# A two-layer hybrid encoder: decay constants on GpSimd, decay by Exp, gates between projection tiles, paired value products

## The chip, the cores and the metric

The kernel runs on one core of one Trainium2 chip. The metric is the device time of one execution in microseconds; the kernel before takes 1383.24 us (median of 3 runs, 1381.23 to 1383.26). TensorE, VectorE (DVE), ScalarE (ACT) and GpSimd (POOL) are the engines that compute, SyncE (SP) issues nearly all loads.

## The reference, cut to what matters

A sequence of 256 tokens of width 1024 goes through two layers in float32. Each layer is a token mixer, a LayerNorm, a channel mixer, a LayerNorm. The channel mixer of the first layer is a dense SwiGLU of width 3584, that of the second the top 2 of 8 SwiGLU experts. The part that the change touches is the mixer, and in it the recurrence:

```
z = x @ W_in -> [conv B | C | h] [c_q | c_kv | k_rope] [lru gate | lru input]
xc  = depthwise_conv4(lru_input) + b
rec = sigmoid(xc @ W_a + b_a);  inp = sigmoid(xc @ W_i + b_i)     (two directions)
log_a = -8 * rec * softplus(-lam)
a = exp(log_a);  u = sqrt(-expm1(2 * log_a)) * inp * xc
h = scan(a, u);  y_lru = gelu(g) * (h_forward + h_backward)
attention: softmax(q k^T) v, 8 heads of 64
y = rms_norm of each group, concatenated, @ W_out
```

The kernel writes sigmoid by Tanh, and with c = 4 softplus(-lam) and s = tanh(c (1 + tanh(ga / 2))) it has a = 2 / (1 + s) - 1 and 1 - a^2 = s (2 / (1 + s))^2 (before), where after the change a = exp(-2c (1 + tanh)) and sqrt(1 - a^2) = sqrt(s) (1 + a).

## The kernel before, in words

All weights stream through a ring of 1 MB tiles (`fresh`, 7 buffers, and a few more in the expert stage) in a fixed order, two pieces of 1024 columns to a tile. A load is issued on SP as soon as the piece order asks for it (`ahead`, `take`) and its buffer is free. Nearly every piece is split into a high part in fp32r, cast by ScalarE (L178) or, for the indices in `HI_POOL`, by GpSimd (L176), and a low part, subtracted by VectorE (L185). A product of two split operands is three matmuls (`mm`, L104). Within the compute part the order is written by hand: `manual_schedule` keeps each engine's instructions in program order, so an instruction that waits holds up all behind it on its engine.

`boundary(i)` is the LayerNorm with the transposition for the next stage. For each of the two blocks of 128 tokens it takes the statistics (`stats`, with the power for the inverse deviation on GpSimd, L249), then applies them: the second half of block 0 on ScalarE and GpSimd (L372 to L375), the rest by two VectorE instructions per half (`centre` L256, `shift` L261). TensorE transposes (`turn`), ScalarE and VectorE copy out (`bring`, L394, L396), and `native` already multiplies the first two raw pieces into the bank `first`. `boundary(0)` also computes the decay constants c of both layers from lam: four operations on GpSimd with a power of e (L279 to L284), and a rational series on VectorE (`decay_rest`, L289 to L302).

`mixer(l)` begins with the convolution of the recurrence's input (L509 to L515), then projects zq 0 and 1, takes the gate weights, `gates(0)`, zq 2, `gates(1)`, Sqrt, two zkv tiles, zkr, and both norms (`rms_scale`, `bcast_cols`). Each `zgroup` takes a piece and runs 24 matmuls. `gates(d)` runs the gate products, four Tanh (L556) and two more Tanh for s (L562). Work of the recurrence is queued in `later` and let in by `tick`: four reciprocals (L575), two gate inputs (L578 to L582), two scans, a sum. Eight projection tiles (`filler`) are spread over the attention's heads. In the loop over heads `scores`, `flip` (the transposition of the probabilities), `softmax`, `normalise` and `values` alternate with them; `values(h)` runs two products of 64 columns, one per 128 keys, into the lower or upper half of a bank.

`dense` and `moe` follow. The expert stage starts with the routing, and its loads (336 tiles) follow in the order of the experts, four light steps of expert 0 first.

Of the kernel before, what the change touches and what calls it, by code (L numbers as in the profile page):

```python
# [29 lines left out]
PIECE = 1024  # L30

PP_CONVW, PP_QG, PP_KVG, PP_LCW, PP_LCB = 0, 6, 9, 11, 19
HI_POOL = (1, 3, 5, 6, 7, 8, 10)
MIX_KINDS = [0] * 2 + [PIECE] * 2 + [0] + [PIECE] * 6 + [768] + [PIECE] * 2 + [768] + [PIECE] * 2 + [768] + [PIECE] * 2 + [768] + [PIECE] * 10

PP_BA, PP_BI, PP_LAM, PP_MG, PP_L = 21, 25, 29, 33, 41
# [45 lines left out]
def hybrid_encoder_kernel(ctx, tc, x_in, pp_in, lnr_in, tab_in, wa_in, wm_in, out):  # L82
# [129 lines left out]
    for b in range(NB):  # L212
        t = state.tile([P, D], F32, name=f"x{b}")
        nc.sync.dma_start(out=t, in_=x_in[b * P:(b + 1) * P, :])
        xs.append(t)

    def load_rows(i, eng=nc.gpsimd):
        t = lnp.tile([P, 2 * D], F32, name="lnrows", tag="lnrows")
# [4 lines left out]
    for j in range(2):  # L223
        nc.sync.dma_start(out=rows0[:, j, 512:], in_=lnr_in[j:j + 1, 512:].to_broadcast([P, 512]))
        rows[0, j] = rows0[:, j, :]
# [6 lines left out]
    G.memset(mhalf, -0.5)  # L232
    ebase = consts.tile([P, 1], F32, name="ebase")
    G.memset(ebase, float(np.e))

    stat = {}

# [32 lines left out]
            shift(b, h, i)  # L270

    cdec = consts.tile([P, 8], F32, name="cdec")
    hbias = consts.tile([P, 2, 8], F32, name="hbias")

    def decay_consts():
        lam = consts.tile([P, 8], F32, name="lam")
        for l in range(2):
            o = l * PP_L
            G.tensor_scalar(lam[:, 4 * l:4 * l + 4], pp[:, o + PP_LAM:o + PP_LAM + 4], -1.0, 0.0, op0=OP.mult, op1=OP.add)  # L279
        na = consts.tile([P, 8], F32, name="nabs")  # L280
        G.tensor_scalar(na, lam, -1.0, 0.0, op0=OP.mult, op1=OP.add)
        V.tensor_tensor(na, na, lam, op=OP.min)
        t = consts.tile([P, 8], F32, name="texp")
        G.tensor_tensor(t, ebase.to_broadcast([P, 8]), na, op=OP.pow)  # L284
        return lam, t

    def decay_rest(lam, t):
        for l in range(2):
            V.tensor_scalar_mul(hbias[:, l, :], pp[:, l * PP_L + PP_BA:l * PP_L + PP_BA + 8], 0.5)  # L289
        s = consts.tile([P, 8], F32, name="sat")  # L290
        V.tensor_scalar_add(s, t, 2.0)
        V.reciprocal(s, s)
        V.tensor_tensor(s, s, t, op=OP.mult)
        z = consts.tile([P, 8], F32, name="zat")
        V.tensor_tensor(z, s, s, op=OP.mult)
        acc = consts.tile([P, 8], F32, name="accat")
        V.tensor_scalar_mul(acc, z, 1.0 / 17.0)
        for k in (15, 13, 11, 9, 7, 5, 3):
            V.scalar_tensor_tensor(acc, acc, 1.0 / k, z, op0=OP.add, op1=OP.mult)
        V.scalar_tensor_tensor(acc, acc, 1.0, s, op0=OP.add, op1=OP.mult)  # L300
        V.tensor_scalar(lam, lam, 0.0, 2.0, op0=OP.max, op1=OP.mult)
        V.scalar_tensor_tensor(cdec, acc, 4.0, lam, op0=OP.mult, op1=OP.add)  # L302

    def boundary(i, final=None, router=False):
        def stats(b):
# [57 lines left out]
        def keep(q):  # L363
            src, dh, dl = views(1, q)
            A.copy(dh, src)
            V.tensor_tensor(dl, src, dh.bitcast(F32), op=OP.subtract)

        stats(0)
        if final is None:
            stats(1)  # L370
        x = xs[0][:, 512:]
        A.activation(x, x, AF.Identity, bias=stat[0][2])  # L372
        A.activation(x, x, AF.Copy, scale=stat[0][1])
# [1 line left out]
        G.tensor_tensor(x, x, rows[i, 1][:, 512:], op=OP.add)  # L375
        centre(0, 0, i)
        shift(0, 0, i)
        if final is not None:
            stats(1)
        if router:  # L380
            turn(0, 0)
            turn(0, 1)
# [20 lines left out]
            native(0, y0, (1, 2))  # L403
        centre(1, 0, i)
        shift(1, 0, i)
        if i == 0:
            decay = decay_consts()
        centre(1, 1, i)
        shift(1, 1, i)
        if i == 0:  # L410
            decay_rest(*decay)
        if not router:
            for q in range(4):
                src, dh, dl = views(0, q)
# [46 lines left out]
    def mixer(l, xT, pz):  # L461
# [5 lines left out]
        with tc.tile_pool(name=f"mix{l}", bufs=1) as mx:  # L467
# [42 lines left out]
            for i in range(2):  # L510
# [35 lines left out]
            def gates(d, wgate):  # L546
                th = []
                for kind in range(2):
                    pg = bank("pg")
                    for i in range(2):  # L550
                        g0 = ((d * 2 + kind) * 2 + i) * P
                        T.matmul(pg[:, i * S:(i + 1) * S], lhsT=wgate[:, g0:g0 + P], rhs=xc[:, i * S:(i + 1) * S],
                                 start=i == 0, stop=True, skip_group_check=True)
                    t = tmp(f"th{kind}")
                    for i in range(2):
                        A.activation(t[:, i * S:(i + 1) * S], pg[:, i * S:(i + 1) * S], AF.Tanh,  # L556
                                     scale=0.5, bias=hbias[:, l, kind * 4 + d * 2 + i:kind * 4 + d * 2 + i + 1])
                    th.append(t)
                s = th[0]
                for i in range(2):  # L560
                    c = cdec[:, 4 * l + 2 * d + i:4 * l + 2 * d + i + 1]
# [8 lines left out]
            hsum = []  # L570

            def queue_recurrence():
                def inv(d, i):
                    sl = slice(i * S, (i + 1) * S)
                    V.reciprocal(rs[d][:, sl], rs[d][:, sl])  # L575

                def gate_input(d):
                    s, u, r = ss[d], us[d], rs[d]  # L578
                    V.scalar_tensor_tensor(u, u, 1.0, xc, op0=OP.add, op1=OP.mult)
                    G.tensor_tensor(s, s, r, op=OP.mult)  # L580
                    G.tensor_tensor(u, u, s, op=OP.mult)
                    G.tensor_scalar(r, r, 2.0, -1.0, op0=OP.mult, op1=OP.add)  # L582

                def scan(d):
                    u, r, h = us[d], rs[d], ss[d]
# [10 lines left out]
                    hsum.append(ss[0])  # L596

                for d in range(2):
                    for i in range(2):
                        later.append(lambda d=d, i=i: inv(d, i))  # L600
# [8 lines left out]
            def filler(i, between=None):  # L609
# [28 lines left out]
                elif i == 5:  # L638
                    gx2 = tmp("gx2")
                    A.activation(gx2, pz, AF.Square)  # L640
                    gh = tmp("gh")
                    A.activation(gh, pz, AF.Copy, scale=0.5)
# [12 lines left out]
            gates(1, wgate)  # L655
            for d in range(2):
                A.activation(ss[d], ss[d], AF.Sqrt)
            queue_recurrence()
            zkv(0)
            tick()  # L660
            zkv(1)
            tick()
            pz = bank("zkr")
            zgroup(pz[0:64, 0:S], m=64)
            kr = tmp("kr", (64, S), tag="kr", bufs=1)
# [17 lines left out]
                    V.tensor_tensor(q, pq[:, 0:S], tq, op=OP.mult)  # L683
                    qs[h] = q

            rq = rms_scale(qsq, 384, "q")
            rkv = rms_scale(kvsq, 256, "kv")
            tick()
            filler(0)
# [89 lines left out]
                A.copy(pT, pt)  # L779
                pTs[h] = pT  # L780

            yms, msq, po = [], [], [None]

            def values(h):
                k = h % 2
                if k == 0:
                    po[0] = bank("po")
                pT = pTs.pop(h)
                for j in range(NB):
                    T.matmul(po[0][64 * k:64 * k + 64, 0:S], lhsT=vt[:, j, h * 64:(h + 1) * 64],  # L790
                             rhs=pT[:, j * S:(j + 1) * S], start=j == 0, stop=j == NB - 1,
                             skip_group_check=True)
                if k == 1:
                    yms.append(scaled_pair("ym", po[0][:, 0:S], col(PP_MG + 2 + h // 2), msq))

            acc = None

# [710 lines left out]
```

## Time and profile before

| | |
|---|---|
| median of 3 runs | 1383.24 us (1381.23 to 1383.26) |
| the profiled execution | 1380.96 us |
| its span | 1379.3 us |
| busy: PE, PEld | 1343.9 us (97%), 966.6 us (70%) |
| busy: DVE, ACT, POOL | 840.6 us (61%), 671.6 us (49%), 173.0 us (13%) |
| moved by DMA | 437.73 MB, mean 317 GB/s |

PE is TensorE's matmuls, PEld its weight loads. Times of the timeline are microseconds from the span's start. A timeline row gives start, duration, engine, line, operation, output and inputs, shape and count, and in brackets how long the engine was idle before it and what ended that. Instructions of one kind in a row are merged. A float32 matmul appears as two passes.

### The profile page before, as it was taken

The page shows a single profiled execution, that of the slowest core. Times are in us where ns is not written, and L with a number is a line of the kernel's source. Part 1 is how long each engine was busy: PE and PEld are TensorE (multiplying, and loading weights), DVE is VectorE, ACT ScalarE, POOL GpSimd, SP SyncE. Part 2 cuts the span into 40 slices and gives each one's busy share as a digit, 9 for nine tenths or more (in the row PEclk, how much of TensorE's full clock was granted, in tenths as well). Part 3 has the DMA queues.
Part 4 walks back from the last instruction along what each step waited for, and adds up shares of the span by engine and source line. Part 5 has one row for each costly group of instructions (what it writes and reads, how often), then busy time and mean ns, then how long its engine had stood idle before and what let it go on. Part 6 is the DMA issues. An engine that isn't in the chain of part 4 may idle for free. (4 is left out here: it accounts for less than half of the span.)

```text
span 1379.3 us, 18986 instructions
## 1 busy us (share of the span) xinstructions
PE 1343.9 (97%) x7199; PEld 966.6 (70%) x7199; DVE 840.6 (61%) x1019; ACT 671.6 (49%) x954; POOL 173.0 (13%) x169
## 2 busy tenths in 40 slices
PE   6999999999999999999999999999999999999995
PEld 5987999999998883556665556666655666655674
DVE  7886644444589771455654555655645656544896
ACT  3763544444355621455444445554445545444674
POOL 4623311111164320000000000000000000000011
PEclk9999999999999999999999999999999999999998
DMA  8442655555074357999999999999999999999980
GB/s 324 165 179 92 228 200 184 184 184 183 31 287 151 159 208 303 421 421 421 420 421 421 421 421 421 421 421 421 420 421 421 421 421 421 421 421 409 419 356 33
DMA packets 61735, 437.73 MB, mean 317 GB/s; under 512 B 6850, under 2 KB 6978, under 8 KB 9284
## 3 DMA queue, kind: packets, MB, share of 16 engines
q1 hardware_dynamic: 60484, 432.25, 77.4%
q0 software_dynamic: 1152, 4.19, 0.9%
q8 instruction: 58, 0.95, 0.3%
q14 instruction: 41, 0.34, 0.1%
HBM read 435.37 MB, written 1.05 MB: 316 GB/s over the span
## 5 line engine op out<-in xcount | busy, mean ns | idle before, releaser
L185 DVE TENSOR_TENSOR lo<-w,hi 128x1024 fp32r<-128x1024 f32 (+1 forms) x474 | 571.1, 1244 | 55.4 <-ACT hi L178 53.3
L178 ACT CAST hi<-w 128x1024 fp32r<-128x1024 f32 (+1 forms) x462 | 471.5, 1046 | 140.8 <-DMA w<-in_wm_dram 57.0
L104 PE MATMUL gu<-hi,xg 128*128 128x512 f32 x896 | 295.6, 399 | 0.0
L1200 PE MATMUL gu<-w,xgl 128*64 128x512 f32 x896 | 205.3, 596 | 0.0
L104 PEld LDWEIGHTS gu<-hi,xg 128*128 128x128 f32 x896 | 168.6, 188 | 42.5 <-ACT hi L178 2.0
L104 PE MATMUL gu<-lo,xg 128*128 128x512 f32 x448 | 176.9, 395 | 0.2 <-DVE lo L185 0.2
L104 PE MATMUL py<-hi,hT 128*128 128x512 f32 x448 | 147.7, 400 | 0.0
L1200 PEld LDWEIGHTS gu<-w,xgl 128*64 128x64 f32 x896 | 60.9, 137 | 112.0 <-issue 110.8
L1116 ACT CAST hT<-pht 128x512 fp32r<-128x512 f32 x28 | 16.4, 585 | 230.3 <-PE pht L1111 230.3
L104 PE MATMUL gu<-xT_hi,hi 128*128 128x256 f32 x432 | 122.2, 283 | 0.0
L104 PE MATMUL gu<-xT_lo,hi 128*128 128x256 f32 x432 | 122.1, 283 | 0.0
L104 PE MATMUL gu<-xT_hi,lo 128*128 128x256 f32 x432 | 122.0, 282 | 0.0
L104 PEld LDWEIGHTS py<-hi,hT 128*128 128x128 f32 x448 | 84.3, 188 | 34.4 <-ACT hi L178 13.8
L1125 PE MATMUL py<-w,hTl 128*64 128x512 f32 x448 | 102.2, 598 | 0.0
L104 PEld LDWEIGHTS gu<-lo,xg 128*128 128x128 f32 x448 | 84.5, 189 | 18.8 <-DVE lo L185 0.5
L1117 DVE TENSOR_TENSOR hT<-pht,hT 128x512 fp32r<-128x512 f32 x28 | 19.3, 691 | 126.3 <-ACT hT L1116 126.3
L104 PE MATMUL py<-lo,hT 128*128 128x512 f32 x224 | 89.3, 399 | 2.4 <-DVE lo L185 2.3
L1215 DVE TENSOR_TENSOR h<-h,gu 128x512 f32<-128x512 f32 x28 | 19.2, 686 | 105.8 <-PE gu L104 105.8
L104 PEld LDWEIGHTS gu<-xT_hi,hi 128*128 128x128 f32 x432 | 82.6, 191 | 1.2
L104 PEld LDWEIGHTS gu<-xT_lo,hi 128*128 128x128 f32 x432 | 82.6, 191 | 1.0
L104 PEld LDWEIGHTS gu<-xT_hi,lo 128*128 128x128 f32 x432 | 82.7, 191 | 0.0
L1279 POOL TENSOR_TENSOR xl<-acc,xh 128x1024 fp32r<-128x1024 f32 x2 | 5.8, 2896 | 556.1 <-ACT xh L1278 556.1
(333 smaller groups left out, 1765.9 us busy)
## 6 DMA issues: line engine op xcount, KB each, us to landing
w<-in_wm_dram SPq DMA_DIRECT2D x336, 1024.0 KB, 15.9
w<-in_wa_dram SPq DMA_DIRECT2D x73, 1024.0 KB, 4.8
lnrows<-in_lnr_dram POOLq DMA_DIRECT2D x6, 512.0 KB, 5.2
x<-in_x_dram SPq DMA_DIRECT2D x2, 512.0 KB, 4.0
rows<-in_lnr_dram POOLq DMA_DIRECT2D x2, 512.0 KB, 10.5
out_dram<-z SPq DMA_DIRECT2D x4, 256.0 KB, 2.8
tab<-in_tab_dram SPq DMA_DIRECT2D x2, 320.0 KB, 7.5
lnrows<-in_lnr_dram SPq DMA_DIRECT2D x2, 256.0 KB, 6.4
```

Source lines behind the costliest of these rows:

```text
L104: T.matmul(dst, lhsT=a, rhs=b, start=start and i == 0, stop=stop and i == len(terms) - 1, skip_group_check=True)
L178: A.copy(hi[:, :kind], src[:, :kind])
L185: V.tensor_tensor(*todo, op=OP.subtract)
L1116: A.copy(hT[:, 0, :], pt)
L1117: V.tensor_tensor(hT[:, 1, :], pt, hT[:, 0, :].bitcast(F32), op=OP.subtract)
L1125: T.matmul(py[0][k * CAP:(k + 1) * CAP, :], lhsT=hp[:, j * CAP:(j + 1) * CAP], rhs=w[:, sl], start=first and j == 0, stop=last and j == 3, ...
L1200: T.matmul(pb[i * CAP:(i + 1) * CAP, :], lhsT=self.unit.xg[:, c, :], rhs=w[:, k * 512:(k + 1) * 512], start=c == 0, stop=c == DC - 1, skip ...
L1215: V.tensor_tensor(self.h, self.h, self.pgu[1], op=OP.mult)
L1279: G.tensor_tensor(xl[:, b], acc[0][:, b], xh[:, b].bitcast(F32), op=OP.subtract)
```

## The change

It does the following.

- At the start tile 0 of the weights is loaded behind x0, ahead of the second halves of the first LayerNorm's rows and of x1. `stats(1)` stands behind the first half of block 0 in every boundary.
- `decay_first` and `decay_rest` run on GpSimd alone, the reciprocal as a power of -1; the latter stands behind the last `keep`. It also makes cneg = -2 cdec.
- `HI_POOL` loses the indices 1 (a piece that isn't cast) and 3, so piece 3 of both mixers is cast on ScalarE.
- The convolution's taps stand behind zq 0 and zq 1, one half each. The order is then: gate weights, zq 2, `gates(0)`, zkv 0, `gates(1)`, zkv 1, Sqrt, the q norm, zkr.
- The decay is an Exp on ScalarE. The reciprocals and GpSimd's r are gone, the gate input is three VectorE operations, and two ticks between the zkv tiles are gone. GeLU's factor is 0.25.
- `values` does nothing for an even head and runs both heads of a pair at an odd one, alternating between the two halves of the bank.

```diff
-HI_POOL = (1, 3, 5, 6, 7, 8, 10)
+HI_POOL = (5, 6, 7, 8, 10)
...
         nc.sync.dma_start(out=t, in_=x_in[b * P:(b + 1) * P, :])
         xs.append(t)
+        if b == 0:
+            ahead(1)
+            for j in range(2):
+                nc.sync.dma_start(out=rows0[:, j, 512:], in_=lnr_in[j:j + 1, 512:].to_broadcast([P, 512]))
+                rows[0, j] = rows0[:, j, :]
...
+            G.tensor_scalar(hbias[:, l, :], pp[:, o + PP_BA:o + PP_BA + 8], 0.5, 0.0, op0=OP.mult, op1=OP.add)
         na = consts.tile([P, 8], F32, name="nabs")
-        G.tensor_scalar(na, lam, -1.0, 0.0, op0=OP.mult, op1=OP.add)
-        V.tensor_tensor(na, na, lam, op=OP.min)
+        G.tensor_scalar(na, lam, 0.0, -2.0, op0=OP.max, op1=OP.mult)
+        G.tensor_tensor(na, na, lam, op=OP.add)
         t = consts.tile([P, 8], F32, name="texp")
         G.tensor_tensor(t, ebase.to_broadcast([P, 8]), na, op=OP.pow)
...
+        G.tensor_scalar(s, t, 1.0, 2.0, op0=OP.mult, op1=OP.add)
+        G.tensor_tensor(s, s, mone.to_broadcast([P, 8]), op=OP.pow)
+        G.tensor_tensor(s, s, t, op=OP.mult)
+        return lam, s
+    def decay_rest(lam, s):
...
+        G.tensor_scalar(acc, z, 1.0 / 17.0, 1.0 / 15.0, op0=OP.mult, op1=OP.add)
+        for k in (13, 11, 9, 7, 5, 3, 1):
+            G.tensor_tensor(acc, acc, z, op=OP.mult)
+            G.tensor_scalar(acc, acc, 1.0, 1.0 / k, op0=OP.mult, op1=OP.add)
...
         stats(0)
-        if final is None:
-            stats(1)
...
         shift(0, 0, i)
-        if final is not None:
-            stats(1)
+        stats(1)
...
         for q in range(4):
             keep(q)
+        if i == 0:
+            decay_rest(*decay)
...
-                    A.activation(s[:, i * S:(i + 1) * S], s[:, i * S:(i + 1) * S], AF.Tanh, scale=c, bias=c)
-                r = tmp("r")
-                G.tensor_scalar(r, s, 1.0, 1.0, op0=OP.mult, op1=OP.add)
+                    c = cneg[:, k:k + 1]
+                    A.activation(r[:, sl], s[:, sl], AF.Exp, scale=c, bias=c)
+                    c = cdec[:, k:k + 1]
+                    A.activation(s[:, sl], s[:, sl], AF.Tanh, scale=c, bias=c)
...
                     V.scalar_tensor_tensor(u, u, 1.0, xc, op0=OP.add, op1=OP.mult)
-                    G.tensor_tensor(s, s, r, op=OP.mult)
-                    G.tensor_tensor(u, u, s, op=OP.mult)
-                    G.tensor_scalar(r, r, 2.0, -1.0, op0=OP.mult, op1=OP.add)
+                    V.scalar_tensor_tensor(s, r, 1.0, s, op0=OP.add, op1=OP.mult)
+                    V.tensor_tensor(u, u, s, op=OP.mult)
...
             zq(0)
+            lru_taps(0)
             zq(1)
+            lru_taps(1)
             wgate = take()
+            zq(2)
             gates(0, wgate)
-            zq(2)
+            zkv(0)
             gates(1, wgate)
+            zkv(1)
             for d in range(2):
                 A.activation(ss[d], ss[d], AF.Sqrt)
             queue_recurrence()
-            zkv(0)
-            tick()
-            zkv(1)
-            tick()
+            rq = rms_scale(qsq, 384, "q")
...
             def values(h):
-                k = h % 2
-                if k == 0:
-                    po[0] = bank("po")
-                pT = pTs.pop(h)
+                if h % 2 == 0:
+                    return
+                po = bank("po")
+                pair = [pTs.pop(h - 1), pTs.pop(h)]
                 for j in range(NB):
-                    T.matmul(po[0][64 * k:64 * k + 64, 0:S], lhsT=vt[:, j, h * 64:(h + 1) * 64],
-                             rhs=pT[:, j * S:(j + 1) * S], start=j == 0, stop=j == NB - 1,
-                             skip_group_check=True)
+                    for k, pT in enumerate(pair):
+                        g = (h - 1 + k) * 64
+                        T.matmul(po[64 * k:64 * k + 64, 0:S], lhsT=vt[:, j, g:g + 64],
+                                 rhs=pT[:, j * S:(j + 1) * S], start=j == 0, stop=j == NB - 1,
+                                 skip_group_check=True)
```

## Rows read from the trace of the kernel before

**Rows 1.** Busy time by stretch: us, busy (instructions) of each engine, PEclk, DMA share, GB/s.

```profile
500.00:530.00 30.00, 29.52 (x190) 20.76 (x188) 16.66 (x48) 9.21 (x22) 6.93 (x9) 1.00 0.51 185
530.00:1310.00 780.00, 777.60 (x3519) 468.28 (x3517) 440.10 (x455) 374.25 (x448) 1.37 (x3) 1.00 1.01 420
```

**Rows 2.** Waits of PE over the run: us in total, times, longest.

```profile
PE pt L776 <- DVE pe L768: 3.1, 2, 1.6
PE bc_q L457 <- POOL rrs_q L451: 1.5, 2, 0.8
```

**Rows 3.** Timeline of PE, first boundary and first mixer.

```profile
14.92 3.11 PE L330 MATMUL first<-xTf,w 128*128 128x128 f32 x16
24.02 4.57 PE L330 MATMUL first<-xTf,w 128*128 128x128 f32 x24 [3.33 <-DVE xTf L396]
28.35 0.36 PE L104 MATMUL zq<-xT_hi,hi 128*128 128x256 f32 x1
49.82 0.36 PE L104 MATMUL zf<-xT_hi,hi 128*128 128x256 f32 x1
```

**Rows 4.** Timelines of DVE and PE: what waits for x0 and for weight tile 0.

```profile
5.23 1.29 DVE L241 BATCH_NORM_STATS2 stats<-x 128x6 f32<-128x512 f32 x2 [5.23 <-DMA x<-in_x_dram]
...
12.22 2.05 PE L330 MATMUL first<-xTf,w 128*128 128x128 f32 x8 [0.82 <-DMA w<-in_wa_dram]
```

**Rows 5.** Timeline of DVE, first boundary and start of the first mixer.

```profile
10.15 1.76 DVE L256 SCALAR_TENSOR_TENSOR x<-x,mv,lnrows 128x512 f32<-128x512 f32 x1
14.20 0.75 DVE L256 SCALAR_TENSOR_TENSOR x<-x,mv,lnrows 128x512 f32<-128x512 f32 x1
19.29 3.86 DVE L299 SCALAR_TENSOR_TENSOR accat<-accat,zat 128x8 f32<-128x8 f32 x7
31.93 1.53 DVE L514 SCALAR_TENSOR_TENSOR xc<-lxp,pp,xc 128x256 f32<-128x256 f32 x3
33.38 1.22 DVE L185 TENSOR_TENSOR lo<-w,hi 128x1024 fp32r<-128x1024 f32 x1
```

**Rows 6.** Timeline of POOL, the same stretch.

```profile
9.73 1.62 POOL L374 TENSOR_TENSOR x<-x,lnrows 128x512 f32<-128x512 f32 x1
13.00 0.79 POOL L279 TENSOR_SCALAR lam<-pp 128x4 f32<-128x4 f32 x2
14.37 2.10 POOL L284 TENSOR_TENSOR texp<-ebase,nabs 128x8 f32<-128x8 f32 x1 [0.28 <-DVE nabs L282]
16.44 2.78 POOL L416 TENSOR_TENSOR xT_lo<-xTf,xT_hi 128x256 fp32r<-128x256 f32 x4
20.29 2.05 POOL L176 TENSOR_SCALAR hi<-w 128x1024 fp32r<-128x1024 f32 x2
```

**Rows 7.** ACT: timeline of the first mixer, and by line all loads for L760 and L1212.

```profile
41.45 1.08 ACT L562 ACTIVATE th<-th,cdec 128x256 f32<-128x256 f32 x2
42.55 1.28 ACT L657 ACT_TABLE_LOAD   x1
43.85 1.36 ACT L657 ACTIVATE th<-th 128x512 f32<-128x512 f32 x2
...
L760 ACT ACT_TABLE_LOAD  x2: 1283/1283/1283, 67.9 to 431.9; - x2
...
L1212 ACT ACT_TABLE_LOAD  x1: 1283/1283/1283, 527.0 to 527.0; - x1
```

**Rows 8.** DVE by line: duration ns min/median/max, first and last start us.

```profile
L575 DVE RECIPROCAL r<-r x8: 1732/1738/1744, 45.6 to 425.4; 128x256 f32<-128x256 f32 x8
```

**Rows 9.** Timeline of PE: value products, products of a light expert, flip of head 7.

```profile
78.12 1.08 PE L790 MATMUL po<-pT,vt 128*64 128x256 f32 x4
...
531.43 4.03 PE L1200 MATMUL gu<-w,xgl 128*64 128x512 f32 x18
...
117.67 0.66 PE L776 MATMUL pt<-ident,pe 128*128 128x128 f32 x4
```

**Rows 10.** Timeline of DVE: end of head 7's softmax in the first mixer.

```profile
116.21 1.37 DVE L768 TENSOR_SCALAR pe<-pe,sm 128x256 f32<-128x256 f32 x2
```

More of the change, by code (lines that the diff above doesn't have):

```diff
@@ L221, in load_rows @@
             eng.dma_start(out=rows[i, j], in_=lnr_in[2 * i + j:2 * i + j + 1, :].to_broadcast([P, D]))
-    for j in range(2):
-        nc.sync.dma_start(out=rows0[:, j, 512:], in_=lnr_in[j:j + 1, 512:].to_broadcast([P, 512]))
-        rows[0, j] = rows0[:, j, :]
     pp = consts.tile([P, PP_N], F32, name="pp")
@@ L234, in hybrid_encoder_kernel @@
     G.memset(ebase, float(np.e))
+    mone = consts.tile([P, 1], F32, name="mone")
+    G.memset(mone, -1.0)
     stat = {}
@@ L272, in hybrid_encoder_kernel, with decay_first @@
     cdec = consts.tile([P, 8], F32, name="cdec")
+    cneg = consts.tile([P, 8], F32, name="cneg")
     hbias = consts.tile([P, 2, 8], F32, name="hbias")
-    def decay_consts():
+    def decay_first():
         lam = consts.tile([P, 8], F32, name="lam")
@@ L283, in decay_consts @@
         t = consts.tile([P, 8], F32, name="texp")
         G.tensor_tensor(t, ebase.to_broadcast([P, 8]), na, op=OP.pow)
[L285 to L289, printed above, removed]
         s = consts.tile([P, 8], F32, name="sat")
-        V.tensor_scalar_add(s, t, 2.0)
-        V.reciprocal(s, s)
-        V.tensor_tensor(s, s, t, op=OP.mult)
+        G.tensor_scalar(s, t, 1.0, 2.0, op0=OP.mult, op1=OP.add)
@@ L294, in decay_rest @@
+        G.tensor_tensor(s, s, mone.to_broadcast([P, 8]), op=OP.pow)
+        G.tensor_tensor(s, s, t, op=OP.mult)
+        return lam, s
+    def decay_rest(lam, s):
         z = consts.tile([P, 8], F32, name="zat")
-        V.tensor_tensor(z, s, s, op=OP.mult)
+        G.tensor_tensor(z, s, s, op=OP.mult)
         acc = consts.tile([P, 8], F32, name="accat")
-        V.tensor_scalar_mul(acc, z, 1.0 / 17.0)
-        for k in (15, 13, 11, 9, 7, 5, 3):
-            V.scalar_tensor_tensor(acc, acc, 1.0 / k, z, op0=OP.add, op1=OP.mult)
@@ L300, in decay_rest @@
-        V.scalar_tensor_tensor(acc, acc, 1.0, s, op0=OP.add, op1=OP.mult)
-        V.tensor_scalar(lam, lam, 0.0, 2.0, op0=OP.max, op1=OP.mult)
-        V.scalar_tensor_tensor(cdec, acc, 4.0, lam, op0=OP.mult, op1=OP.add)
+        G.tensor_scalar(acc, z, 1.0 / 17.0, 1.0 / 15.0, op0=OP.mult, op1=OP.add)
+        for k in (13, 11, 9, 7, 5, 3, 1):
+            G.tensor_tensor(acc, acc, z, op=OP.mult)
+            G.tensor_scalar(acc, acc, 1.0, 1.0 / k, op0=OP.mult, op1=OP.add)
+        G.tensor_tensor(acc, acc, s, op=OP.mult)
@@ L304, in boundary @@
+        G.tensor_scalar(lam, lam, 0.0, 2.0, op0=OP.max, op1=OP.mult)
+        G.tensor_scalar(acc, acc, 4.0, 0.0, op0=OP.mult, op1=OP.add)
+        G.tensor_tensor(cdec, acc, lam, op=OP.add)
+        G.tensor_scalar(cneg, cdec, -2.0, 0.0, op0=OP.mult, op1=OP.add)
     def boundary(i, final=None, router=False):
@@ L405, in boundary @@
         shift(1, 0, i)
-        if i == 0:
-            decay = decay_consts()
         centre(1, 1, i)
@@ L410, in boundary @@
         if i == 0:
-            decay_rest(*decay)
+            decay = decay_first()
         if not router:
@@ L509, in mixer, with lru_taps @@
             A.copy(lxp[:, :, 1:S + 1], pz.rearrange("p (c t) -> p c t", c=2))
-            for i in range(2):
+            def lru_taps(i):
                 d = xc[:, i * S:(i + 1) * S]
@@ L558, in gates @@
                     th.append(t)
-                s = th[0]
+                s, r = th[0], tmp("r")
                 for i in range(2):
-                    c = cdec[:, 4 * l + 2 * d + i:4 * l + 2 * d + i + 1]
-                    A.activation(s[:, i * S:(i + 1) * S], s[:, i * S:(i + 1) * S], AF.Tanh, scale=c, bias=c)
-                r = tmp("r")
-                G.tensor_scalar(r, s, 1.0, 1.0, op0=OP.mult, op1=OP.add)
+                    k = 4 * l + 2 * d + i
+                    sl = slice(i * S, (i + 1) * S)
+                    c = cneg[:, k:k + 1]
+                    A.activation(r[:, sl], s[:, sl], AF.Exp, scale=c, bias=c)
+                    c = cdec[:, k:k + 1]
+                    A.activation(s[:, sl], s[:, sl], AF.Tanh, scale=c, bias=c)
                 V.tensor_scalar_max(s, s, 1e-30)
@@ L572, in queue_recurrence @@
             def queue_recurrence():
-                def inv(d, i):
-                    sl = slice(i * S, (i + 1) * S)
-                    V.reciprocal(rs[d][:, sl], rs[d][:, sl])
                 def gate_input(d):
@@ L598, in queue_recurrence @@
                 for d in range(2):
-                    for i in range(2):
-                        later.append(lambda d=d, i=i: inv(d, i))
                     later.append(lambda d=d: gate_input(d))
@@ L641, in filler @@
                     gh = tmp("gh")
-                    A.activation(gh, pz, AF.Copy, scale=0.5)
+                    A.activation(gh, pz, AF.Copy, scale=0.25)
                     G.tensor_scalar(gx2, gx2, 0.044715, 1.0, op0=OP.mult, op1=OP.add)
@@ L684, in keep_q @@
                     qs[h] = q
-            rq = rms_scale(qsq, 384, "q")
             rkv = rms_scale(kvsq, 256, "kv")
@@ L780, in flip @@
                 pTs[h] = pT
-            yms, msq, po = [], [], [None]
+            yms, msq = [], []
             def values(h):
-                k = h % 2
-                if k == 0:
-                    po[0] = bank("po")
-                pT = pTs.pop(h)
+                if h % 2 == 0:
+                    return
+                po = bank("po")
+                pair = [pTs.pop(h - 1), pTs.pop(h)]
                 for j in range(NB):
-                    T.matmul(po[0][64 * k:64 * k + 64, 0:S], lhsT=vt[:, j, h * 64:(h + 1) * 64],
-                             rhs=pT[:, j * S:(j + 1) * S], start=j == 0, stop=j == NB - 1,
-                             skip_group_check=True)
-                if k == 1:
-                    yms.append(scaled_pair("ym", po[0][:, 0:S], col(PP_MG + 2 + h // 2), msq))
+                    for k, pT in enumerate(pair):
[3 more added lines that the diff above has]
+                                 skip_group_check=True)
+                yms.append(scaled_pair("ym", po[:, 0:S], col(PP_MG + 2 + h // 2), msq))
             acc = None
```

## The prediction

> **What bounds the kernel now.** I read the busy time by stretch first. In the expert stage, from 530 us to 1310 us, the DMA engines are full (share 1.01, 420 GB/s) and TensorE is busy 777.6 of 780 us; in the 30 us before it the DMA share is only 0.51 [rows 1]. So the weight buffers are full when the experts begin, the loads wait for them to be released, and from then on the stage runs at the speed of its transfers. Nothing in it is edited, so it takes as long as before and starts earlier or later by what the stages ahead of it win or lose. This is why a microsecond of TensorE time in a boundary or a mixer counts in full.
>
> In those stages TensorE hardly stands still. The list of its waits, over the whole run, names 3.1 us for the softmax on VectorE (L768) and 1.5 us for GpSimd's power of the q norm (L451), both over the two mixers [rows 2]; its timeline adds 3.33 us for a copy on VectorE (L396) in the first boundary. That timeline also gives the marks for the sums: the first mixer's projection zq begins at 28.35 and its first filler (zf), behind both norms, at 49.82 [rows 3].
>
> **The change part by part.** The sum is made against the profiled execution, 1380.96 us (span 1379.3), which is 2.28 us below the median 1383.24.
>
> *Startup.* Tile 0 of the weights is loaded ahead of the second halves of the first norm's rows and of x1. x0 landed at 5.2 us, and tile 0, the last of these transfers, just before TensorE's first product at 12.22 stopped waiting for it [rows 4]. At 420 GB/s its 1 MB are 2.5 us, so it comes at about 7.7 now, and x1, the last in its place, at about 12. So x1's statistics, moved behind the first half of x0, run from 12.0 to 13.8, and its four STTs of 0.75 end at 16.9. VectorE's decay chain, which stood ahead of the L396 copy until 23.5 (seven of its operations alone took 3.86), is gone from that queue [rows 5]. The second half of x0 waits for its late rows and GpSimd's two products of 1.6 [rows 6] and is ready at 13, as before. TensorE's 16 matmuls on it began at 14.92 for 3 us and 10.4 us later zq began, 3.33 of them a wait [rows 3]; they can begin at 14.1 now, as nothing is left to wait for in between but the transposes. So zq could begin at 17 + 6 = 23 and not 28.35: 5.3 us won.
>
> *What gives it back.* On GpSimd the constants are now ten operations, two of them powers, then (behind the xT_lo subtractions) 21 more, and only behind those the memsets of lxp and the casts of pieces 5 and 6, which were done at 22.3 [rows 6]. VectorE's subtraction of piece 5 stands ahead of cq0's low half and of all conv taps, which were moved behind the projections. Two small operations took 0.79, the first beside a VectorE STT, about 0.2 and 0.6; a power over 8 columns 2.10 [rows 6]. I take 0.25, nearer the undisturbed one, since VectorE has nothing left to do while it waits. The chain: x1's rstd until 14.4; 8 x 0.25 + 2 x 2.1 = 6.2, 20.6; four subtractions, 2.78 before, up to 4.3 beside VectorE, say 3.5, 24.1; 21 x 0.25, 29.4; the cast of piece 5 1.03, 30.4; its subtraction on VectorE 1.22, 31.7. Then cq0 (0.5), the first half's taps (0.4 + 1.53), lo of piece 6, cq1 and the second half's taps [rows 5]: 6.1, so xc is complete at 37.8 and the first gates end at 39.1. Two zkv, the second gates, zkr and two norms are 11 us of unbroken TensorE work: zf at 50.3 against 49.82, **+0.5**. With 0.16 per small operation and shorter powers the same chain gives 46 (-3.8), with 0.30 and the slower subtractions 52.3 (+2.5).
>
> *rms_q.* The q norm now goes ahead of zkr, so its power is done under 2.7 us of matmuls and the wait for it ends: **-1.5** in two mixers [rows 2]. If another wait takes its place, 0.
>
> *Exp and the gates on ScalarE.* Each mixer gets four more activations of some 0.54 (two in 1.08), 2.2 us. Sqrt with its table load (1.28 + 1.36) moves behind both kv squares, so in the first mixer the squares come no later than now. The second mixer finds Silu's table in ScalarE. Before, Tanh ran from it without a load; Exp will not, since Silu behind the softmax needed a load of its own (L1212) [rows 7]. So a load of 1.28 is added ahead of the second mixer's gates. ScalarE's work from the gates to the second kv square is then 11.4 us beside 10.6 us of TensorE, their sum on GpSimd another 1 to 1.8, and rms_kv waits: **+1.2** (0 to 2.5). In the rows the activation behind a load starts 1.30 us after the load began. The Trainium skill (ScalarE: Activation LUTs, What ACT_TABLE_LOAD costs) counts a drain of about 1.38 us with every switch. By that the estimate would be 1.4 us more; the rows show no drain, and I go by them.
>
> *Reciprocals and products.* VectorE loses four reciprocals of 1.74 (7.0 us) [rows 8] in each mixer and gets two more operations of 512 columns per direction instead, some 2.8 us going by an STT of 0.75 [rows 5], which GpSimd loses. Over 4 us of its backlog before the first softmax go, more than the 1.55 us that TensorE waits there in each mixer: **-3.1** (bounds 0 and -3.4).
>
> *Value products.* A head's two products are four passes, 1.08 us from the first's start to the last's end, 1.0 with the overlap into the next instruction; there are 16 heads. In the expert stage two 64-column products on alternating halves run beside each other: 18 passes of 512 columns take 4.03 us, 0.43 to 0.45 a pair, 0.22 for 256 columns [rows 9]. So a pair of heads takes about 1.0 instead of 2.0: eight pairs, -8.0. But the product of head 6 now stands behind the flip of head 7, and that flip follows its softmax at once: VectorE ends it at 117.58, TensorE flips at 117.67 [rows 9, 10]. There about 0.9 per mixer comes back as a wait: **-6.2** (bounds -4 and -8).
>
> At nothing: the cast of piece 3 on ScalarE (under the wait for x1's rows; without that cover 1.05 more before y1 in each of two boundaries), the r and products that GpSimd loses, the 0.25 scale.
>
> **Sum.** +0.5 - 1.5 + 1.2 - 3.1 - 6.2 = -9.1: 1371.9, and with the 2.3 us of the median 1374.1.
>
> **Rivals.**
> 1. *The startup gain stays.* GpSimd's chain is short enough and zq, gates and zkv run on from 23 us: the first term is -3.8 or better, down to -5.3, and the sum -13.4 to -15: 1369. For it: a tiny operation at 0.2. Against: 31 operations with two powers stand ahead of the cast.
> 2. *Slower: the constants on GpSimd hold up the first mixer.* At the disturbed 0.63 for each of the 29 small operations the chain is 29 x 0.38 = 11 us longer, with the slow subtractions some 12, and the sum +3: 1386. It decides from 0.25 + 9.1 / 29 = 0.56 us per operation. For it: VectorE's own tiny operations took 0.55 beside GpSimd, and an STT of 0.75 took 1.76 while GpSimd multiplied [rows 5, 6]. Against: most of the 21 run while VectorE waits for them. The Trainium skill (SBUF — State Buffer, Who interferes with whom) says that a VectorE instruction with two SBUF inputs and a GpSimd read exclude each other for a whole instruction. By that rule this rival is the outcome wherever VectorE stays busy; the stretched STT agrees with it.
> 3. *The alternation does not pay*; a pair's four products still go one behind the other. Without its -6.2 the sum is -2.9, 1380.3. Against: the pairs of rows 9.
> 4. *The expert stage hides it*: its transfers end when they ended before, 1383. Against: the DMA share of 0.51 ahead of it [rows 1].
> 5. *Exp and Tanh swap tables each time*: 16 loads, 20 us of ScalarE, half of it on the path, 1393. Against: the softmax has one load in each mixer, though GeLU's Tanh (L645) lies between its Exps [rows 7].
>
> **How the numbers follow.** Forecast 0.60, rivals 0.20, 0.06, 0.07, 0.06, 0.01. A measurement of this kernel tells about 0.2% (2.8 us) from no change. Faster by more: forecast, rival 1 and half of rival 3, 0.83; within: the other half and rival 4, 0.10; slower 0.07. The forecast's own best case (-3.8, -1.5, 0, -3.4, -8) is -16.7, 1366.5; its worst (+2.5, 0, +2.5, 0, -4) is +1. Such ends seldom meet, so the range goes from 1366 to 1381, with rivals 1 and 3 inside.
>
> **What would show it.** Right: zq at about 23, VectorE's L185 waiting for GpSimd's cast near 30, zf near 50, no wait of pt for pe in the first softmax, value products of about 1.0 per pair with a wait of pt before the last pair, one more table load in the second mixer, an expert stage of 780 us as before. Wrong: zf below 47 or above 53, products in single file, an expert stage that grows by what the mixers win.

## The result and the profile after

The changed kernel takes 1373.78 us (median of 5 runs, 1373.27 to 1374.96) against 1381.62 us (1381.14 to 1383.26, 5 runs) for the one before on the same chip: ratio 0.9944, 95% interval 0.9933 to 0.9954, so 7.8 us faster. The profiled execution took 1373.78 us, its span is 1372.1 us against 1379.3, 7.2 less. Of all runs in this document one, of the version with the old start, was slow (1441.6 us at a mean granted clock of 0.883) and is left out. Five marks on TensorE's timeline split the spans: the first zf of each mixer, the first product of the dense layer (gu), the first zq of the second mixer, and pxg, the first product of the experts. The stretch of a mixer from zq to zf is called its front below.

| stretch | before | after | difference | forecast |
|---|---|---|---|---|
| start to zf, first mixer | 49.82 | 55.27 | +5.45 | +0.5 |
| zf to the dense layer | 97.44 | 90.88 | -6.56 | -5.4 |
| dense layer to zq, second mixer | 244.25 | 244.27 | 0 | 0 |
| zq to zf, second mixer | 22.27 | 24.12 | +1.85 | +1.2 |
| zf to pxg | 98.67 | 92.12 | -6.55 | -5.4 |
| pxg to the end | 866.8 | 865.4 | -1.4 | 0 |

(The forecast for a stretch behind zf is half of -1.5, -3.1 and -6.2.) The last line isn't a gain of the change: in all twelve kernels of this study, which share the expert stage, it lies between 865.2 and 867.1. The marks of the kernel before that [rows 3] doesn't show:

```profile
147.26 0.36 PE L104 MATMUL gu<-xT_hi,hi 128*128 128x256 f32 x1
391.51 0.36 PE L104 MATMUL zq<-xT_hi,hi 128*128 128x256 f32 x1
413.78 0.36 PE L104 MATMUL zf<-xT_hi,hi 128*128 128x256 f32 x1
512.45 0.33 PE L990 MATMUL pxg<-oh,xh 128*128 128x128 f32 x1
```

The total came out near the forecast, but the stretch up to the first zf is 5.0 us worse than forecast, and the two stretches behind a zf are 2.3 us better together. The timeline of TensorE in the changed kernel, with the marks, the last flip and a pair of value products:

```profile
20.55 0.37 PE L104 MATMUL zq<-xT_hi,hi 128*128 128x256 f32 x1
55.27 0.36 PE L104 MATMUL zf<-xT_hi,hi 128*128 128x256 f32 x1
116.65 0.55 PE L776 MATMUL pt<-ident,pe 128*128 128x128 f32 x3 [0.34 <-DVE pe L768]
119.89 1.08 PE L792 MATMUL po<-pT,vt 128*64 128x256 f32 x8
146.15 0.36 PE L104 MATMUL gu<-xT_hi,hi 128*128 128x256 f32 x1
390.42 0.36 PE L104 MATMUL zq<-xT_hi,hi 128*128 128x256 f32 x1
414.54 0.36 PE L104 MATMUL zf<-xT_hi,hi 128*128 128x256 f32 x1
506.66 0.33 PE L991 MATMUL pxg<-oh,xh 128*128 128x128 f32 x1
```

Against [rows 3], zq starts 7.8 us earlier and zf 5.45 us later. Eight passes of the value products take the time of four in [rows 9]. Busy time by stretch of the changed kernel (columns as in [rows 1]):

```profile
524.00:1304.00 780.00, 778.49 (x3524) 469.59 (x3524) 441.87 (x457) 376.36 (x450) 1.48 (x3) 1.00 1.01 422
20.55:55.27 34.72, 26.42 (x172) 24.58 (x170) 18.04 (x23) 15.25 (x32) 17.38 (x38) 0.85 0.54 211
29.00:34.00 5.00, 1.62 (x6) 1.33 (x7) 2.93 (x3) 0.75 (x1) 4.75 (x10) 0.69 0.46 192
34.00:39.00 5.00, 4.51 (x22) 4.11 (x21) 4.86 (x8) 0.75 (x2) 1.94 (x3) 0.62 0.00 0
39.00:44.00 5.00, 2.76 (x7) 2.23 (x8) 4.78 (x6) 0.84 (x2) 1.91 (x2) 0.72 0.11 21
41.19:55.27 14.08, 14.03 (x95) 13.29 (x95) 7.33 (x10) 11.49 (x24) 1.78 (x2) 0.88 0.57 200
```

The experts run as before, at the speed of their transfers. The front of the first mixer does not: TensorE is busy 26.42 of 34.72 us, and its mean granted clock is 0.85, since parts of the front run at the lower of its two levels, 1.2 GHz in place of 2.4. (The last row goes from the moment when xc is complete to zf.) What TensorE waits for in the front (pg is the bank of the gate products):

```profile
PE zq L104 <- POOL hi L176: 3.1, 1, 3.1
PE pg L557 <- DVE xc L519: 2.7, 1, 2.7
PE zq L104 <- DVE lo L185: 1.3, 1, 1.3
PE zq L104 <- POOL xT_lo L418: 1.2, 1, 1.2
```

All four, 8.3 us, go back to GpSimd's queue, two of them by way of VectorE. Its timeline in the changed kernel:

```profile
14.13 0.20 POOL L284 TENSOR_SCALAR lam<-pp 128x4 f32<-128x4 f32 x1
...
16.87 1.67 POOL L290 TENSOR_TENSOR texp<-ebase,nabs 128x8 f32<-128x8 f32 x1
...
20.63 0.78 POOL L294 TENSOR_TENSOR sat<-sat,texp 128x8 f32<-128x8 f32 x1
21.37 2.80 POOL L418 TENSOR_TENSOR xT_lo<-xTf,xT_hi 128x256 fp32r<-128x256 f32 x4
24.13 0.20 POOL L299 TENSOR_TENSOR zat<-sat 128x8 f32<-128x8 f32 x1
24.42 0.20 POOL L301 TENSOR_SCALAR accat<-zat 128x8 f32<-128x8 f32 x1
...
29.98 4.04 POOL L176 TENSOR_SCALAR hi<-w 128x1024 fp32r<-128x1024 f32 x3
...
34.72 1.22 POOL L176 TENSOR_SCALAR hi<-w 128x1024 fp32r<-128x1024 f32 x1
...
39.70 1.22 POOL L176 TENSOR_SCALAR hi<-w 128x1024 fp32r<-128x1024 f32 x1
```

And VectorE's, in both mixers:

```profile
31.07 2.05 DVE L185 TENSOR_TENSOR lo<-w,hi 128x1024 fp32r<-128x1024 f32 x1 [9.72 <-POOL hi L176]
...
34.20 2.52 DVE L519 SCALAR_TENSOR_TENSOR xc<-lxp,pp,xc 128x256 f32<-128x256 f32 x3
...
38.62 2.57 DVE L519 SCALAR_TENSOR_TENSOR xc<-lxp,pp,xc 128x256 f32<-128x256 f32 x3
...
398.83 2.59 DVE L519 SCALAR_TENSOR_TENSOR xc<-lxp,pp,xc 128x256 f32<-128x256 f32 x3
```

The 21 small operations are 0.285 us from start to start, the cast follows them at 29.98 (forecast 29.4), and the subtraction of that piece ends at 33.1 (forecast 31.7). The taps, 1.53 in [rows 5], take 2.5 while GpSimd casts (34.72, 39.70) and adds squares of the q norm, so xc is complete at 41.2 and not at 37.8.

### The profile page after: what moved, and what is told of

The parts are those of the page before. It is cut to its first block, busy times and chain, and to the rows that moved or that the text cites. A ratio compares the mean times of both kernels' runs of the same rounds, so it can differ in the third digit from the quotient of the medians.

```text
span 1372.1 us, 18977 instructions
## 1 busy us (share of the span) xinstructions
PE 1335.9 (97%) x7199; PEld 963.8 (70%) x7199; DVE 825.2 (60%) x1001; ACT 679.5 (50%) x965; POOL 158.1 (12%) x179
## 5 line engine op out<-in xcount | busy, mean ns | idle before, releaser
L178 ACT CAST hi<-w 128x1024 fp32r<-128x1024 f32 x464 | 473.5, 1047 | 131.3 <-PE gu L104 55.3
L104 PE MATMUL dacc<-hi,hp 128*128 128x512 f32 x224 | 74.2, 394 | 0.1
```

What stands on the lines that cost most here:

```text
L104: T.matmul(dst, lhsT=a, rhs=b, start=start and i == 0, stop=stop and i == len(terms) - 1, skip_group_check=True)
L178: A.copy(hi[:, :kind], src[:, :kind])
```

## The experiments

Each edit is made to the changed kernel, and each kernel is compared with runs of the one before on its own chip.

**The later part of the constants behind the casts.**

```diff
-            decay_rest(*decay)
+            pending.append(decay)
...
             zq(0)
+            if pending:
+                decay_rest(*pending.pop())
             lru_taps(0)
```

> The changed kernel with decay_rest (21 small GpSimd operations, 5.8 us there) moved behind the casts of pieces 5 and 6, into the first mixer behind zq 0. Theory 1 (GpSimd's queue holds the first mixer): the cast of piece 5 starts near 24 instead of 30, zq 2 no longer waits 3.1 us for it, xc is complete near 34 instead of 41, and the filler zf starts at about 48 instead of 55.3; time about 7 us less than the changed kernel's 1373.8, so 1367. Theory 2 (the taps' new place behind the projections on VectorE is what delays the gates): the gates still wait for xc, zf not before 53, time 1372 to 1374.

1365.46 us, ratio 0.9884 (0.9869 to 0.9898). zf comes at 47.25, 8.0 us earlier, and every stretch behind it is as in the changed kernel within 0.3 us, so all of it reaches the end: theory 1 holds. The front, GpSimd's casts and VectorE's taps:

```profile
20.55:47.25 26.70, 23.64 (x171) 22.27 (x170) 17.30 (x23) 15.26 (x31) 21.60 (x38) 0.94 0.62 241
```

```profile
24.29 2.09 POOL L176 TENSOR_SCALAR hi<-w 128x1024 fp32r<-128x1024 f32 x2
```

```profile
28.20 1.52 DVE L521 SCALAR_TENSOR_TENSOR xc<-lxp,pp,xc 128x256 f32<-128x256 f32 x3
...
31.61 1.53 DVE L521 SCALAR_TENSOR_TENSOR xc<-lxp,pp,xc 128x256 f32<-128x256 f32 x3
```

The operations moved occupy GpSimd from 24.13 to 29.95, 5.8 us, but 8.0 are won. The casts start 5.7 earlier and are now over before the taps begin, so the taps have only tiny operations beside them and are back at 1.53: xc is complete at 33.1 in place of 41.2. From there to zf 14.1 us pass in both, at a clock of 0.88. Of the 8.0 TensorE's waits give 5.2 and its busy time 2.8 (26.42 to 23.64 us, at a clock of 0.94 for 0.85).

**The series left out.** This separates the length of the chain from what runs beside the taps.

```diff
-        for k in (13, 11, 9, 7, 5, 3, 1):
+        for k in ():
```

> The fourteen operations of the series in the later part of the decay constants are left out, so cdec is not the reference's; seven operations of that part remain, in their place ahead of the memsets and the casts of pieces 5 and 6. Theory 1 (each small operation on GpSimd holds the casts, and with them zq and zf, by the 0.285 us that the trace shows between two starts, and TensorE's idle time then costs a lower granted clock on top): the cast of piece 5 starts 4.0 us earlier than at 29.98, zf falls by more than that, 4.5 to 6, to 49.3 to 50.8, the granted clock between the two marks rises above 0.85, and the time is 1368 to 1369.5. Theory 2 (the clock's part is nothing, each microsecond on GpSimd is one at zf): zf at 51.2, 1369.8. Theory 3 (the taps, not the casts, set the gates): zf falls by less than 2.

1370.46 us, ratio 0.9915 (0.9902 to 0.9929). The cast starts 4.1 us earlier, but zf, at 51.96, comes only 3.3 earlier: more than theory 3 allowed, and less than one for one, so theories 1 and 2 both miss. The rows of GpSimd, of VectorE, and the busy time from xc to zf:

```profile
25.86 4.06 POOL L176 TENSOR_SCALAR hi<-w 128x1024 fp32r<-128x1024 f32 x3
...
30.62 1.22 POOL L176 TENSOR_SCALAR hi<-w 128x1024 fp32r<-128x1024 f32 x1
...
34.33 1.08 POOL L176 TENSOR_SCALAR hi<-w 128x1024 fp32r<-128x1024 f32 x1
```

```profile
30.10 2.54 DVE L519 SCALAR_TENSOR_TENSOR xc<-lxp,pp,xc 128x256 f32<-128x256 f32 x3
...
34.54 2.18 DVE L519 SCALAR_TENSOR_TENSOR xc<-lxp,pp,xc 128x256 f32<-128x256 f32 x3
```

```profile
36.72:51.96 15.24, 15.19 (x95) 14.44 (x95) 7.33 (x10) 11.48 (x24) 1.79 (x2) 0.80 0.56 207
```

Casts still lie beside the taps, which take 2.54 and 2.18, and the wait of pg for xc grows to 3.4 us. Even so xc is complete at 36.7, 4.5 us earlier than in the changed kernel, so up to there nothing is lost. The loss of 1.2 lies behind xc, where TensorE is busy throughout: its 95 matmuls take 15.24 us at a granted clock of 0.80, against 14.08 at 0.88. The clock went to its lower level at the end of that longer wait, and stayed there from 36 to beyond 42 us. So there are three costs. One is the length of GpSimd's chain. The second is the casts beside the taps: in the first experiment, where none lies beside them, xc came 8.1 us earlier for 5.7 at the casts' start. The third is the clock behind the stalls.

**All constants behind the casts.**

```diff
-        if i == 0:
-            decay = decay_first()
...
             zq(0)
+            if pending:
+                pending.pop()
+                decay_rest(*decay_first())
             lru_taps(0)
```

> All the decay constants, the ten first operations too, stand behind the casts of pieces 5 and 6. Theory 1 (what GpSimd has ahead of those casts sets zf, one for one until another wait ends last): the xT_lo subtractions are done by about 17 us and the casts by about 20, the wait of zq for xT_lo (1.3) and the wait of pg for xc (1.8) that the version with only the later part moved still has go, zf falls from its 47.25 to 44 to 45.5, and the time is 1361.5 to 1364. Theory 2 (from here TensorE's own work and the constants' end set the gates: the whole chain now runs until about 34 us beside VectorE and the Exp waits for it): zf stays at 47 or later, the time at 1365 to 1368, with the wait moved to rms_kv or to pg.

1365.47 us, ratio 0.9884 (0.9869 to 0.9900). zf falls to 45.26, as theory 1 said, but zq starts 1.2 us later and the median is that of the first experiment, as theory 2 said. The front, and GpSimd's rows:

```profile
21.72:45.26 23.54, 22.14 (x172) 21.05 (x170) 15.29 (x21) 14.48 (x31) 19.31 (x37) 1.00 0.57 219
```

```profile
14.07 4.13 POOL L418 TENSOR_TENSOR xT_lo<-xTf,xT_hi 128x256 fp32r<-128x256 f32 x4
...
18.25 1.04 POOL L176 TENSOR_SCALAR hi<-w 128x1024 fp32r<-128x1024 f32 x1
```

The subtractions of xT_lo now run beside VectorE's products on x1 (1.1 to 1.2 us each where one took 0.75 in [rows 5]), and that delays zq. Of the 2.0 us won at zf 0.4 are lost before the dense layer and 0.6 in the dense layer and its boundary, 0.4 of the latter as one more wait of the transposition for VectorE; why, no run shows. The waits in the front are down to 1.4 us. With the clock at 1.00 throughout, the front's matmuls are busy 22.14 us. The changed kernel's 34.72 us are these 22.1, the 8.3 of waits listed above, and 4.3 more of busy time (26.42 - 22.14) at the lower clock.

**The taps ahead of the projections.**

```diff
+            lru_taps(0)
+            lru_taps(1)
             zq(0)
-            lru_taps(0)
             zq(1)
-            lru_taps(1)
```

> The changed kernel with both halves of the convolution's taps ahead of zq 0 again, as before the change. Theory 1 (GpSimd's queue): the taps still wait for the memsets of lxp, which stand behind decay_rest at 29.9, so zq 2 waits for the low part of piece 5 even longer, but xc is complete some 3 us earlier; zf in the first mixer between 53 and 56. In the second mixer the wait of the gates for xc (1.6 us) goes. Time 1370 to 1373. Theory 2 (the taps' place): zf at about 48, and the time 1365 to 1367.

1373.87 us, ratio 0.9942 (0.9929 to 0.9955), no difference. The wait of pg for xc is gone and zq waits up to 6.3 us for the low part of piece 5 in its place; zf comes at 56.21. In the second mixer the front falls from 24.12 to 23.38. zf is about where theory 1 put it, the time a little above its forecast. In the first mixer the order on VectorE only decides who waits for GpSimd.

**The old start.** The loads of tile 0 and the late rows, and the place of `stats(1)`, are as before.

```diff
-        if b == 0:
-            ahead(1)
-            for j in range(2):
...
         stats(0)
+        if final is None:
+            stats(1)
```

> The changed kernel with the old order of the first loads and the old place of the second block's statistics. Theory 1 (GpSimd's queue sets the first gates, not the start of zq): zq starts up to 2 us later than 20.55, but the cast of piece 5 starts where GpSimd's chain puts it, within 1 us of 30, and zf stays at 54 to 56; time 1373 to 1375. Rival (the startup's gain reaches the end): zf and the time move by as much as zq, 1375.5 or more.

1375.73 us (1375.03 to 1376.22, 5 runs), ratio 0.9956 (0.9943 to 0.9969). zq starts 3.0 us later and zf 0.4 earlier, and the cast of piece 5 starts at the same moment as in the changed kernel:

```profile
29.98 4.05 POOL L176 TENSOR_SCALAR hi<-w 128x1024 fp32r<-128x1024 f32 x3
```

So for zf theory 1 holds: the earlier zq brings nothing while the casts hold it. The time is the rival's, though: the median is 2.0 us above the changed kernel's. The intervals overlap, but none of the five runs is as fast as the slowest of the changed kernel. The trace, which is of the fastest of them, has 1.7 us more behind pxg (867.1) and none in the mixers; where the others lose their time isn't shown.

**The value products one head at a time.**

```diff
-                if h % 2 == 0:
-                    return
...
+                    T.matmul(po[0][64 * k:64 * k + 64, 0:S], lhsT=vt[:, j, h * 64:(h + 1) * 64],
```

> The changed kernel with the value products of each head by themselves, as before the change. If the alternation overlaps two products: 16 products of 1.0 instead of 8 pairs of 1.0, less 0.9 to 1.3 per mixer that the pairing gives back as waits: 5.5 to 6.5 us more than 1373.8, about 1379.8. If it doesn't overlap: no change, 1373.8.

1381.51 us, ratio 0.9995 (0.9986 to 1.0004): without the pairs nothing is left of the gain. Both stretches behind zf grow by 3.52 us (94.40, 95.64), and a head takes what a pair took:

```profile
80.15 1.08 PE L790 MATMUL po<-pT,vt 128*64 128x256 f32 x4
```

So the pairing is worth 7.0 us in the trace, somewhat more than expected. What it gives back can be read off the changed kernel: before the last flip TensorE waits 0.25 and 0.34 us for the softmax of head 7, and the output projection (acc) waits 0.5 for yn, of which the version without pairs has neither.

**The reciprocals back in place of Exp.**

```diff
-                    A.activation(r[:, sl], s[:, sl], AF.Exp, scale=c, bias=c)
...
+                G.tensor_scalar(r, s, 1.0, 1.0, op0=OP.mult, op1=OP.add)
...
+                    V.reciprocal(rs[d][:, sl], rs[d][:, sl])
...
+            tick(2)
             pz = bank("zkr")
```

> Exp undone alone: r = 1 + t on GpSimd, its reciprocal on VectorE (four operations of 1.74 us in each mixer) and the old gate input come back, two of the queued steps standing ahead of zkr; the decay constants, the tiles of the first boundary, the place of the norms and the paired value products stay as in the changed kernel. Theory 1 (the wait of the first softmax, 1.5 us in each mixer, was VectorE's backlog with the reciprocals in it): pt waits 2.5 to 3.5 us for pe in all again, the stretch from zf to the dense layer and its like in the second mixer grow by 1.3 to 1.8 us each, and the time is 1376 to 1377.5. Theory 2 (the earlier q norm or the order of the queued steps removed that wait): both stretches within 0.4 us of 90.88 and 92.12, time 1373 to 1374.5.

1378.56 us (1377.67 to 1381.24, 7 runs), ratio 0.9976 (0.9964 to 0.9987), 4.8 above the changed kernel. The profiled execution was the longest of the seven; in it the two stretches behind zf grow by 3.44 and 3.48 us, twice what I expected; the second front is 0.63 shorter, without the load for Exp. Waits of TensorE from 55 to 150 us (pt is the bank of the transposed probabilities, bc_kv that of the kv norm's factors), and VectorE's row:

```profile
PE pt L783 <- DVE pe L775: 2.1, 3, 1.6
PE bc_kv L461 <- POOL rrs_kv L455: 1.2, 1, 1.2
```

```profile
53.02 3.35 DVE L581 RECIPROCAL r<-r 128x256 f32<-128x256 f32 x2
```

Theory 1 holds in kind, not in size. TensorE waits 1.6 for the first softmax again, as in [rows 2], and 1.2 for the kv norm, whose small operation on VectorE stands behind the two reciprocals. The place of the q norm didn't remove a wait; with reciprocals in the queue the wait goes to the other norm.

**The q norm behind zkr.**

```diff
-            rq = rms_scale(qsq, 384, "q")
             pz = bank("zkr")
...
+            rq = rms_scale(qsq, 384, "q")
             rkv = rms_scale(kvsq, 256, "kv")
```

> The q norm alone goes back behind zkr, next to the kv norm; no reciprocal comes back. Theory 1 (my term of -1.5: its place ahead of zkr hides its power): bc_q waits for rrs_q again, about 0.75 in each mixer, both stretches from the first zf onward (90.88 and 92.12) grow by 0.6 to 0.9, and the time is 1375 to 1375.5. Theory 2 (in the kernel before it was the reciprocals on VectorE, ahead of the norms' small operations, that made this wait, and in the version with the reciprocals it appeared at the kv norm instead): under 0.3 in each mixer, time 1373.3 to 1374.5.

1374.81 us (1372.13 to 1375.49), ratio 0.9947 (0.9933 to 0.9960), no difference. No wait for rrs_q returns; the stretches behind zf are 90.85 and 92.15, the second front 24.13. Theory 2 holds for both stretches; the time lies between the two forecasts. (zf of the first mixer is 1.2 us later, with 0.6 more of the wait for xc and 0.6 more of busy time at a clock of 0.81; in versions that edit nothing ahead of it, it lies between 54.9 and 55.7.)

**Tanh in place of Exp.**

```diff
-                    A.activation(r[:, sl], s[:, sl], AF.Exp, scale=c, bias=c)
+                    A.activation(r[:, sl], s[:, sl], AF.Tanh, scale=c, bias=c)
```

> The four Exp of each direction pair are replaced by Tanh with the same operands, so the decay factor r is not the one of the reference; the number and size of ScalarE's activations stay, and only the extra table load of 1.28 us in the second mixer should go. Theory 1 (in the second mixer's front the conv taps on VectorE, stretched to 2.6 us beside GpSimd, set the gates, not ScalarE): the stretch from the first zq to the first zf of the second mixer stays within 0.5 us of the changed kernel's 24.12, the wait of rms_kv for the squares shrinks by no more than its 0.4 to 0.5 us, and the time is 1373 to 1374.5. Theory 2 (my prediction's term of +1.2: the load and the activations on ScalarE delay rms_kv): the stretch shortens by 1.2 to 1.8 us and the time is about 1372.

1373.27 us, ratio 0.9934 (0.9920 to 0.9947). The second front is 23.48 us, 0.64 less, and no wait of rms_kv is left: between the two theories. ScalarE in the changed kernel, at the load that this version lacks:

```profile
403.93 1.28 ACT L569 ACT_TABLE_LOAD   x1
405.23 0.60 ACT L569 ACTIVATE r<-th,cneg 128x256 f32<-128x256 f32 x1
```

The load exists and costs half of its 1.28 us; the rest of it is hidden. The waits of the changed kernel from 390 to 414.6 us say what the other part is (the first of them was 0.3 in the kernel before; rms_kv is the bank of the kv norm's sums):

```profile
PE pg L557 <- DVE xc L519: 1.6, 1, 1.6
PE rms_kv L450 <- POOL ckvsq L494: 0.4, 1, 0.4
```

**Taps of the second mixer half moved**, on top of all constants late.

```diff
+            if l == 1:
+                lru_taps(0)
             zq(0)
...
-            lru_taps(0)
+            if l == 0:
+                lru_taps(0)
```

> As the one with all constants late, and in the second mixer alone the conv taps of the first half stand ahead of the first projection, those of the second half behind the second one as before. Theory 1 (there the taps beside GpSimd set the gates, 1.6 us of wait of pg for xc): the stretch from the first zq to the first zf of the second mixer falls from 24.1 to 22.4 to 23.4, and the time by 0.7 to 1.7 us against the other. Theory 2 (the low part of the next piece behind the taps is then as late): zq waits for L185 in place of pg, within 0.4 us.

1363.86 us (1363.80 to 1364.17), ratio 0.9869 (0.9854 to 0.9884), the lowest of all, 9.9 us below the changed kernel. The second front falls from 23.94 to 23.10. VectorE's second half of taps, and the wait for it in the second front:

```profile
389.32 2.18 DVE L519 SCALAR_TENSOR_TENSOR xc<-lxp,pp,xc 128x256 f32<-128x256 f32 x3
```

```profile
PE pg L557 <- DVE xc L519: 0.7, 1, 0.7
```

It was 1.6, and the taps took 2.59. Theory 1 holds: there too the taps set the gates. How much of that is their place in the order and how much the casts beside them, this run doesn't separate.

## Why the prediction was right, and where it was not

The sum, -9.1, met a measured -7.8, and the forecast's mechanism is the one that happened: the startup's gain is taken by GpSimd's chain, and the gain comes from the attention. That the total came so near is partly luck. In the trace the stretch up to the first zf is 5.0 us worse than forecast and the second front 0.65, the stretches behind zf are 2.3 better, and 1.4 came from the last stretch, which the change doesn't touch: -7.2 for -9.1. The terms one by one:

*Startup.* Mis-sized, and zq came earlier: it started at 20.55, not 23. (The working doesn't give 23 either: 17 and the 10.4 less 3.33 of the rows are 24.) The 16 matmuls began at 13.03, not 14.1, no wait followed, and the last matmuls ahead of zq ran at a clock of 1.00, where in the kernel before it was 0.61 from 24.02 to 28.35, behind the wait. None of this reached zf: the old start has the same zf.

*What gives it back, +0.5: the step that was mis-sized, by 5 us.* GpSimd's part of the chain was right: 29.98 for 29.4, with a small operation at 0.285 for 0.25 (0.2 busy alone, about 0.7 beside VectorE), and powers of 1.67 and 1.64 for 2.1. Three things behind it were not. VectorE's subtraction took 2.05 and each half's taps about 1 us more than the rows of before, which I had used although in them GpSimd cast nothing at that point (+3.4 at xc, with the 0.6 of GpSimd). The Trainium skill (SBUF — State Buffer, Who interferes with whom) says that a VectorE instruction with two SBUF inputs contends with a GpSimd instruction that reads; I had quoted it for the slower rival alone, and the taps of 1.53 and 2.5 agree with it. Then from xc to zf 12.5 us were forecast and 14.1 passed: I had taken full speed behind the stalls, but the granted clock was 0.88 there, first at the level of 1.2 GHz and then at 2.4, after TensorE had stood still from 38.5 to 41.2. With all constants behind the casts it was 1.00, and the same 95 matmuls were busy 12.8 us for 14.0. The bound of +2.5 (its own terms, 29 x 0.05 and 0.8, come to +2.7) was too narrow for the same reasons; zf above 53 was named as the mark of an error, and it was one. The slower rival's price per operation (0.56) was not reached; its condition, that VectorE and GpSimd disturb each other, was, and this is what cost.

*rms_q, -1.5, and reciprocals, -3.1.* The sum of the two was too small and the split wrong. Without pairs the stretch behind zf is 3.04 us shorter than before (97.44 to 94.40), 6.1 in two mixers for 4.6. The q norm's place is worth nothing by itself: the reciprocals ahead of the norms' operations made that wait as well as the softmax's.

*Exp and ScalarE, +1.2.* +1.85 in the second front. Of it 0.64 is the table load with the wait of rms_kv (0.4) that was my mechanism. The larger part is the wait of pg for xc, 1.6 for 0.3: the taps in their new place, which the forecast didn't price in this mixer.

*Value products, -6.2.* Measured -7.0; the give-back at the last flip was 0.6 rather than 0.9 per mixer. The rival that the alternation doesn't pay fell with the version of single heads.

*The expert stage* passes on what the mixers win or lose: from pxg to the end it is 865.2 to 867.1 us in every version, and the first experiment shows it for 8 us in one step. (The 780 us of the forecast are the length of the window that I chose.) The rival that the startup gain stays describes a kernel that exists: with the constants behind the casts it takes 1365.

## What to carry to other kernels

A chain of tiny operations is best placed behind the large work that other engines wait for on the same queue, not ahead of it; here that alone was worth 8 us, as much as the whole change. Moving its first ten operations as well brought nothing more in the time (1365.47 for 1365.46). When work moves to GpSimd, or VectorE's work moves to where GpSimd is busy, take the durations for both from a row in which both were busy. A stall of TensorE is priced at its length and, where the granted clock falls with it, at the slower matmuls behind it.

## What the runs showed of the hardware that was not expected

A GpSimd operation on 128x8 is busy 0.20 us, but dependent ones start 0.285 us apart; beside VectorE single ones took 0.3 to 1.2. A power over 8 columns took 1.64 to 1.67 in the changed kernel. The same front (172, 171 and 172 matmuls in the traces) was busy 26.42, 23.64 and 22.14 us at granted clocks of 0.85, 0.94 and 1.00. The pairs of value products also freed time beyond their own passes: four pairs save 4 x 1.0 by the rows and cost about 1.1 of waits, yet 3.5 were won, so some 0.6 per mixer lie in the instructions around them; which, was not tried.
